# Nearest-neighbour upsampling on one core: the first load's issue moves from SyncE's DMA queue to ScalarE's

## The chip, the cores and the metric

The kernel runs on one core of one Trainium2 chip. The metric is the device time of one execution in microseconds (us). The kernel before takes 197.63 us, the median of three runs (197.22 to 197.87).

On this core SP (SyncE) and ACT (ScalarE) issue the DMAs of this kernel. The page of the profile lists two DMA queues: q1 carries ten DMAs, as many as SP issues, and q10 two, as many as ScalarE issues. Both are served by the same 16 DMA engines. VectorE (DVE) and ScalarE do the copying inside on-chip memory. TensorE (PE) has no work.

## The reference

Every pixel of a float32 image batch of shape 16 x 64 x 64 x 64 is repeated twice in both directions:

```python
for i in range(new_h):
    for j in range(new_w):
        src_i = i // scale_factor      # scale_factor is 2
        src_j = j // scale_factor
        result[:, :, i, j] = x[:, :, src_i, src_j].copy()
```

16.78 MB are read and 67.11 MB are written.

## The kernel before

The image rows of all batches and channels are one list of 16 x 64 x 64 = 65,536 rows of 64 floats. Each of the 128 partitions holds 512 of them, which follow each other in memory, so one partition's share is 128 KB of input and 512 KB of output. The whole input stays on chip in `xt`, the rear part of one large tile `mem` (lines 186 to 188).

Three loads bring the input, cut by rows (lines 192 to 195): rows 0 to 31 (the "head", 8 KB in a partition), rows 32 to 287 (64 KB) and rows 288 to 511 (56 KB).

The loop in lines 204 to 217 then goes over nine chunks of rows, of 54, 38, 54, 61, 54, 63, 63, 63 and 62 rows. For each chunk

- VectorE expands the first `kv` rows into a buffer inside `mem` (line 213) and ScalarE the others (line 214). In chunk 0 VectorE has 53 rows, so its copy reads rows 0 to 52, and ScalarE only row 53.
- one DMA stores the chunk (line 216). SP issues it, but chunks 3 and 5 are issued by ScalarE (line 215).

The buffers alternate between the front of `mem` and the region just below the rows not yet expanded, which reaches into rows of `xt` that are done with. A buffer is used again once its store has landed, and a region of `xt` once its rows have been expanded. The framework adds the waits for this from the reads and writes; a DMA announces that it has landed through a semaphore.

Every engine first runs a short opening block which ends in a barrier that all engines pass together, and then the body. Two functions edit the finished program. `begin_before_barrier` (line 13) takes SP's first `EARLY` = 3 instructions of the body, which are the three loads, and puts them ahead of SP's drain in the opening block, so that SP issues them before it arrives at the barrier. `close_early` (line 80) rearranges the block at the end, so that only SP waits for the last store. `close_on_gpsimd` is defined but not used.

Of the kernel before, what the change touches and what calls it, by code (L numbers as in the profile page):

```python
# [6 lines left out]

EARLY = 3  # L10


def begin_before_barrier(nc):

    blocks = nc.main_func.blocks
    main, body = blocks[0], blocks[1]
    sp = mybir.EngineType.SP
    loads = [i for i in body.instructions if i.engine == sp][:EARLY]  # L20
    for load in loads:
        assert isinstance(load, mybir.InstDMACopy), type(load)
        assert not (load.sync_info and load.sync_info.on_wait)
    names = [i.name for i in loads]
    body.instructions = [i for i in body.instructions if i.name not in names]
    kept = list(main.instructions)
    at = next(
        n
        for n, i in enumerate(kept)
        if i.engine == sp and isinstance(i, mybir.InstDrain)  # L30
    )
    kept[at:at] = loads
    main.instructions = kept


# [118 lines left out]
@with_exitstack  # L154
def kernel(
    ctx: ExitStack,
    tc: tile.TileContext,
    x: bass.AP,
    scale_factor: int,
    out: bass.AP,  # L160
):
    nc = tc.nc
    nc.at_finalize(begin_before_barrier)
    nc.at_finalize(close_early)
    P = nc.NUM_PARTITIONS
    s = int(scale_factor)
    B, C, H, W = x.shape
    R = B * C * H // P
    fdt = x.dtype

    xp = x.rearrange("b c h w -> (b c h) w").rearrange("(p r) w -> p r w", p=P)
    op = out.rearrange("b c (h hd) w -> (b c h) (hd w)", hd=s).rearrange(
        "(p r) w -> p r w", p=P
    )

    rows = [54, 38, 54, 61, 54, 63, 63, 63, 62]
    GROW = s * s
    FREE = 79
    WF = FREE * GROW * W
    assert sum(rows) == R
    mem_pool = ctx.enter_context(tc.tile_pool(name="mem", bufs=1))
    mem = mem_pool.tile([P, WF + R * W], fdt, name="mem")
    xt = mem[:, WF:].rearrange("p (r w) -> p r w", r=R)

    HEAD = 32
    cuts = [0, HEAD, R // 2 + HEAD, R]
    for lo, hi in zip(cuts, cuts[1:]):
        nc.sync.dma_start(out=xt[:, lo:hi], in_=xp[:, lo:hi])  # L195

    def expanded(r0, r1):
        return (
            xt[:, r0:r1].unsqueeze(2).unsqueeze(4).to_broadcast([P, r1 - r0, s, W, s])
        )  # L200

    r0 = 0
    before = (0, 0)
    for n, k in enumerate(rows):
        size = k * GROW * W
        at = 0 if n % 2 == 0 else WF + r0 * W - size
        assert at >= before[1] or at + size <= before[0]
        before = (at, at + size)
        u = mem[:, at : at + size].rearrange(
            "p (k a w b) -> p k a w b", k=k, a=s, w=W  # L210
        )
        kv = k - 1 if n == 0 else k * 5 // 8 & ~1
        nc.vector.tensor_copy(out=u[:, :kv], in_=expanded(r0, r0 + kv))  # L213
        nc.scalar.copy(out=u[:, kv:], in_=expanded(r0 + kv, r0 + k))  # L214
        issuer = nc.scalar if n in (3, 5) else nc.sync
        issuer.dma_start(out=op[:, r0 : r0 + k, :], in_=u)  # L216
        r0 += k
# [35 lines left out]
```

## Time and profile before

| what | value |
|---|---|
| median of three runs | 197.63 us |
| span of the profiled execution, first to last instruction | 195.7 us |
| VectorE busy | 52.3 us in 9 copies |
| ScalarE busy | 42.1 us in 9 copies and a table load |
| mean DMA rate over the span | 429 GB/s |
| SP's issue of one load | 0.38 to 0.43 us |
| first load, issue to landing | 4.7 us |
| second load, issue to landing | 23.6 us |
| third load, issue to landing | 40.2 us |
| ScalarE's own issues (chunks 3 and 5) | at 74.39 and 109.09 us |

Times inside the profile count from the span's start, which is the start of SP's issue of the first load. An issue is the instruction by which SP or ScalarE hands a transfer to its queue; the transfer starts later, and it has landed when its semaphore is complete. In the rows on windows, the columns are the stretch, its length, the busy time and number of instructions of VectorE, ScalarE and GpSimd, the granted TensorE clock, the DMA share and the GB/s. In the rows on DMA queues, a window counts the packets that start in it, with their MB and the time that they take as a share of 16 engines over the window; this can be over 100% for a short window, since a packet counts whole where it starts. So a short window's GB/s can be over what the engines move.

### The profile page before, as it was taken

What the parts mean: (1) busy time and instruction counts of PE and PEld (TensorE: products, weight loads), DVE (VectorE), ACT (ScalarE), POOL (GpSimd) and SP (SyncE); (2) the same over time, 40 slices, a digit from 0 to 9 for tenths busy, and PEclk for the clock granted to TensorE, in tenths of its full rate; (3) what the DMA queues carried; (4) which work ended last, traced back from release to release, by engine and by line L of the source; (5) the groups of instructions that cost most, each with busy time, mean ns of one, the idle gap of its engine ahead of it and who ended that gap; (6) DMA issues with size and microseconds to landing.
All of it is one profiled execution on the core that took longest, in us unless ns stands there. A gap on an engine that the chain in (4) does not pass through costs nothing.

```text
span 195.7 us, 102 instructions
## 1 busy us (share of the span) xinstructions
DVE 52.3 (27%) x9; ACT 42.1 (21%) x10; POOL 0.2 (0%) x4
## 2 busy tenths in 40 slices
DVE  0000099940026081000627200055540063000000
ACT  2000000150029700000694000059700073000000
POOL 0000000000000000000000000000000000000000
DMA  9999989889898989989999899999999999999994
GB/s 429 429 429 429 402 375 562 375 362 542 362 435 382 540 384 441 490 385 406 408 476 475 362 482 488 416 422 422 422 422 422 422 422 422 435 499 493 428 441 208
DMA packets 1728, 83.89 MB, mean 429 GB/s; under 512 B 192, under 2 KB 192, under 8 KB 192
## 3 DMA queue, kind: packets, MB, share of 16 engines
q1 hardware_dynamic: 1440, 67.63, 80.1%
q10 hardware_dynamic: 288, 16.25, 19.2%
HBM read 16.78 MB, written 67.11 MB: 429 GB/s over the span
## 4 chain that ended last, share of the span: by engine, by line
DMA 65%; ACT 11%; DVE 7%; SPq 0%; issue 0%; DVEq 0%; ACTq 0%
DMA out_dram<-mem 53%; DMA mem<-in_x_dram 12%; ACT mem L214 11%; DVE mem L213 7%; SPq L195 0%; DVEq L213 0%; ACTq L214 0%; SPq L216 0%
## 5 line engine op out<-in xcount | busy, mean ns | idle before, releaser
L213 DVE COPY mem<-mem 128x9728 f32<-128x9728 f32 (+3 forms) x9 | 52.3, 5818 | 111.0 <-DMA out_dram<-mem 86.9
L214 ACT COPY mem<-mem 128x6400 f32<-128x6400 f32 (+5 forms) x9 | 40.8, 4530 | 119.6 <-DMA out_dram<-mem 84.4
L214 ACT ACT_TABLE_LOAD x1 | 1.3, 1283 | 1.7 <-PEq L234 1.7
L234 POOL MEMSET const-bfloat16-1.0<- 128x1 bf16 x1 | 0.1, 101 | 0.0
L234 POOL MEMSET const-uint8-127<- 128x1 uint8 x1 | 0.1, 101 | 0.0
L234 POOL MEMSET const-float32-0.0<- 128x1 f32 x1 | 0.1, 98 | 0.2 <-issue 0.2
L234 POOL MEMSET const-float32-1.0<- 128x1 f32 x1 | 0.1, 98 | 0.0
## 6 DMA issues: line engine op xcount, KB each, us to landing
out_dram<-mem SPq DMA_DIRECT2D x3, 6912.0 KB, 30.1
out_dram<-mem SPq DMA_DIRECT2D x2, 8064.0 KB, 27.8
out_dram<-mem ACTq DMA_DIRECT2D x1, 8064.0 KB, 29.9
out_dram<-mem SPq DMA_DIRECT2D x1, 7936.0 KB, 32.3
out_dram<-mem ACTq DMA_DIRECT2D x1, 7808.0 KB, 29.3
mem<-in_x_dram SPq DMA_DIRECT2D x1, 7168.0 KB, 40.2
out_dram<-mem SPq DMA_DIRECT2D x1, 4864.0 KB, 26.8
mem<-in_x_dram SPq DMA_DIRECT2D x1, 1024.0 KB, 4.7
```

The lines of the kernel that those rows point to most:

```text
L213: nc.vector.tensor_copy(out=u[:, :kv], in_=expanded(r0, r0 + kv))
L214: nc.scalar.copy(out=u[:, kv:], in_=expanded(r0 + kv, r0 + k))
L234: nc = _bacc.Bacc("TRN2", target_bir_lowering=False, num_devices=1)
```

## The change

The first of the three loads is issued by ScalarE in place of SP. `EARLY` becomes a table with a number of loads for each of the two engines, and `begin_before_barrier` moves ScalarE's first DMA of the body ahead of ScalarE's drain in the opening block, and SP's first two ahead of SP's. The sizes of the loads, the copies and the stores stay as they are.

```diff
-EARLY = 3
+EARLY = {mybir.EngineType.Activation: 1, mybir.EngineType.SP: 2}
...
     main, body = blocks[0], blocks[1]
-    sp = mybir.EngineType.SP
-    loads = [i for i in body.instructions if i.engine == sp][:EARLY]
...
     kept = list(main.instructions)
...
+    for engine, early in EARLY.items():
+        loads = [
+            i
+            for i in body.instructions
+            if i.engine == engine and isinstance(i, mybir.InstDMACopy)
+        ][:early]
+        for load in loads:
+            assert not (load.sync_info and load.sync_info.on_wait)
+        names = [i.name for i in loads]
+        body.instructions = [i for i in body.instructions if i.name not in names]
+        at = next(
+            n
+            for n, i in enumerate(kept)
+            if i.engine == engine and isinstance(i, mybir.InstDrain)
+        )
+        kept[at:at] = loads
     main.instructions = kept
...
     for lo, hi in zip(cuts, cuts[1:]):
-        nc.sync.dma_start(out=xt[:, lo:hi], in_=xp[:, lo:hi])
+        issuer = nc.scalar if lo == 0 else nc.sync
+        issuer.dma_start(out=xt[:, lo:hi], in_=xp[:, lo:hi])
```

More of the change, by code (lines that the diff above doesn't have):

```diff
@@ L18, in begin_before_barrier @@
     main, body = blocks[0], blocks[1]
-    sp = mybir.EngineType.SP
-    loads = [i for i in body.instructions if i.engine == sp][:EARLY]
[L21 to L25, printed above, removed]
-    kept = list(main.instructions)
[L27 to L32, printed above, removed]
+    kept = list(main.instructions)
+    for engine, early in EARLY.items():
[14 more added lines that the diff above has]
+        kept[at:at] = loads
     main.instructions = kept
```

## The prediction

> **What bounds the kernel now.** I read the chain of waits first, because it says which kind of work leads from the start to the end.
>
> ```profile
> 24.11 14.30 DVE mem L213
> 38.41 0.02 issue
> 38.42 0.02 SPq L216
> 38.44 0.04 issue
> 38.48 18.96 DMA out_dram<-mem
> ```
>
> (Start in us, length in us, what.) The chain begins with SP's second load, issued at 0.43 and landed 23.58 us later, at 24.01. VectorE's first copy starts at 24.11 and ends at 38.41, SP issues the first store at 38.48, and from there to the end the chain changes between stores and short copies.
>
> Second, the page's rows on the DMA queues: is there idle DMA time that an earlier or later load could use up?
>
> ```profile
> DMA packets 1728, 83.89 MB, mean 429 GB/s; under 512 B 192, under 2 KB 192, under 8 KB 192
> ## 3 DMA queue, kind: packets, MB, share of 16 engines
> q1 hardware_dynamic: 1440, 67.63, 80.1%
> q10 hardware_dynamic: 288, 16.25, 19.2%
> ```
>
> The shares add to 99.3% of the span: the 16 engines idle 0.7% of 195.7, 1.4 us. So the kernel is bound by bytes, and a change can only cost idle time put between packets, or save what is left of the 1.4 us and of a slow ramp. The 12 DMAs have 1728/12 = 144 packets each, nine for each engine; one of the nine is tiny (192 = 12 x 16 under 512 B) and I read it as the semaphore's. q10 carries two DMAs (288/144), as many as ScalarE issues; q1 is SP's queue. A load is thus eight data packets on each engine: 8 KB for the first load (1024 KB / 128 packets), 64 KB for the second and 56 KB for the third.
>
> Third, how an engine chooses between two queues. ScalarE issues a store at 109.09, while SP's store on q1 is running. These are the packets that start in the windows 109.09 to 115.3 and 115.3 to 117.7:
>
> ```profile
> DMA packets 48, 2.80 MB, mean 451 GB/s; under 512 B 0, under 2 KB 0, under 8 KB 0
> q1 hardware_dynamic: 32, 1.77, 65.7%
> q10 hardware_dynamic: 16, 1.03, 38.3%
> ...
> q1 hardware_dynamic: 16, 0.88, 85.0%
> ```
>
> After the issue every engine still starts two packets of q1 (32/16) beside the one that it is running, then one of q10 (16/16), then one of q1 again. ScalarE's other store shows the same: from its issue at 74.39 to 80.7, 33 packets of q1 and 16 of q10 start. So an engine is committed three packets deep, the running one and two more, and then alternates packet by packet.
>
> **The change part by part.** I call the 8 KB packets of the first load B1 to B8, the 64 KB ones of the second A1 to A8, the 56 KB ones of the third C1 to C8; b and a are the semaphore's packets.
>
> Issuing. SP's three issues take 381 to 432 ns each. SP now issues two, so its barrier comes 0.4 us earlier and ScalarE's 0.4 us later than they did (ScalarE's drain stood at 0.1, SP's first issue at 0.00). The barrier released ScalarE at 1.73, and nothing behind it is needed before 24.0. If that cover were gone the sum would be 0.4 us. ScalarE's queue q10 holds nothing else before the store issued at 74.39, and GpSimd's carries none of the DMAs, so no transfer is passed there. No wait is added: VectorE's first copy already waits for two loads. Price: nothing.
>
> First packet. In the first 1.0 us no packet starts; six start in the next 0.1. This delay is now that of A1, issued at 0.00, instead of B1: nothing either way. The window rows show a slow ramp behind it:
>
> ```profile
> 1.00:1.50 0.50, 0.00 (x0) 0.00 (x0) 0.00 (x0) 1.00 1.37 328
> 1.50:2.00 0.50, 0.00 (x0) 0.27 (x1) 0.00 (x0) 1.00 0.77 229
> 2.00:3.00 1.00, 0.00 (x0) 1.00 (x1) 0.00 (x0) 1.00 0.97 410
> 78.80:91.60 12.80, 0.00 (x0) 0.00 (x0) 0.00 (x0) 1.00 1.00 435
> ```
>
> (Last column GB/s.) Against 435 the first two microseconds lose 156/435 + 25/435 = 0.42 us. If 64 KB packets ramp better, between 0 and 0.4 us is saved. The last row is also a stretch in which both queues alternate: interleaving costs no rate.
>
> The order of the first 9 MB: here is the cost. ScalarE's issue starts at 0.1 if it takes the place of its drain, behind SP's A at 0.00, and SP's C follows A at about 0.43. If an idle engine fills its three places as soon as A is there, A1, A2 and A3 are committed before B can be seen. Then it alternates:
>
> A1 A2 A3 B1 A4 B2 A5 B3 A6 B4 A7 B5 A8 B6 a B7 C1 B8 C2 b
>
> Before, b and a both stood ahead of C1. Now two packets of the third load stand ahead of b. The third load landed at 0.9 + 40.2 = 41.1, the second at 24.0, so a C packet takes 17.1/8 = 2.1 us, and the first load lands 2 x 2.1 = 4.2 us later than the second did, at 28.2. VectorE's first copy (53 rows) needs rows of both loads, so it starts at 28.3 rather than 24.11, ends 14.30 later at 42.6, and the first store is issued at 42.7 rather than 38.48. ScalarE's first copy needs row 53 alone, from the second load; its next copy waited 14.0 us for VectorE and slips with it. Nothing else is queued on VectorE.
>
> What the 4.2 us cost. Some of it is covered: the first store was issued at 38.48, but the engines only came free for it between 40.1 and 40.8 (32 packets start in that window, 16 of them tiny). On idle engines its packets would have started after 38.48 + 1.0, by the delay of the first load, which gives 0.6 us of cover on the earliest engine. If a store's first packet comes faster, the cover grows; at no delay it is 40.1 - 38.5 = 1.6. The loads themselves end as early as before, since the bytes ahead are the same. So the idle time is 4.2 - 0.6 = 3.6 at most and 4.2 - 1.6 = 2.6 at least. I take 3.2, nearer to the first, as the only idle start in the trace is the loads'. Afterwards nothing gives it back: from 41 to 195 the window row reads 430 GB/s, so every later store slides by the same amount, with the copies between them.
>
> Sum: 195.7 + 3.2 = 198.9 for the span. The profiled execution's span lies 1.9 below the median of 197.63; I add the same 1.9: **200.8 us**, with 200.2 to 201.2 as this case's own range.
>
> Against this stands the Trainium skill. The page "DMA: Bandwidth & Descriptors", section "Issuing engines are not separate DMA queues", says that issuing from several engines saves only the sequencer's time to issue, since all transfers interleave on the same 16 engines. By that alone the sum would be the 197.4 of the rival below. The trace agrees that rate is unchanged (435 GB/s with both queues), but shows that interleaving moves a transfer's landing.
>
> **The rivals.**
>
> *Order does not bite* (not slower). If B reaches an engine before A, or no more than one A packet ahead of it is taken, the order is B1 A1 B2 A2 or A1 B1 A2 B2, and a and b both still come ahead of C1. Landing stays at 24.0, and half of the 0.4 us ramp gives 197.63 - 0.2 = 197.4. It decides as soon as the three-deep commitment is not filled within the 0.1 us by which SP leads. For it: the lead is tiny; the rows show commitment only on busy engines. Also, what I read as depth might be a delay of some 4 us until a new queue is noticed. Against that: load 1 needed 1.0 us, and both stores found two packets per engine though the engines' packet starts are spread over 2 us.
>
> The same page, section "Queues, rings and completion order", has an engine drain a whole packet of about 9 to 17 descriptors from a ring before it switches. If that packet were all eight of a load's pieces, A would be finished, then B, then C, and the forecast would be this rival's. The trace does not agree: q10 and q1 take turns after 16 pieces, one on each engine.
>
> *Two packets ahead instead of three.* If A1 and A2 alone are taken, b stands behind one C packet: 2.1 us late, less 0.6 to 1.6 of cover: 0.5 to 1.5, about 1.0, so 198.6.
>
> *The load comes much later.* If the first use of ScalarE's queue costs some microseconds, or the move ahead of the barrier does not do what it says and ScalarE issues behind the release at 1.73, the three-deep commitment holds all the more: A4 is chosen when A1 ends, about 3.4. Only a load seen later than that lands another 2.1 us late per A packet: 202.9.
>
> *Ramp and finish gain.* The ramp's whole 0.42 is saved, and the engines finish together: their last tiny packets start between 194.7 and 195.4, some 0.6 us apart, so up to 0.3 more on the average. 197.63 - 0.7 = 196.9. [...] Against it: the same cold start is paid by A1, and the rows do not show that packet size causes it.
>
> **How the numbers follow.** Three ahead 0.5, two ahead 0.13, much later 0.07, order does not bite 0.2, ramp gain 0.1. A difference counts from 0.3%, 0.6 us, about what a measurement of this kernel can tell from no change (its runs lie between 197.22 and 197.87). Slower is the first three, 0.7; same 0.2; faster 0.1. The time is that of the likeliest case, 200.8. The range reaches down to the unchanged order with its whole ramp gain, 197.63 - 0.42 = 197.2, and up to the 3.6 us bound and the 0.2 by which the slowest run lies above the median, 201.4. It leaves out the last rival and the much later load, 0.17.
>
> **What would show it.** On the changed kernel's windows of the first 30 us: q10's first 8 KB packets behind 48 packets of q1 (three on each engine), its tiny packets near 28 rather than ahead of 23.7; VectorE's first copy at about 28.3, released by the load; the first store's issue at 42.7; and a hole in the DMA row between about 40.5 and 43.5. If VectorE still starts near 24.1, commitment was not deep at an idle start, and I am wrong. If it starts late but the DMA row has no hole, the cover was larger than I took. If the times after the hole do not shift by one amount, later stores gave something back.

## The result: 0.16% slower, with the order unharmed

| | before | changed |
|---|---|---|
| median of 21 runs each | 197.47 us | 197.75 us |
| ratio, 95% interval | | 1.0016 (1.0010 to 1.0022) |
| profiled execution, span | 195.7 us | 196.7 us |

The forecast was 200.8 and slower. The kernel is 0.28 us slower, less than the 0.3% that was to count. What happened is the first rival, "order does not bite", without the small gain that it included.

The chain of waits of the changed kernel (start, length, what):

```profile
0.11 24.35 DMA mem<-in_x_dram
24.47 0.02 issue
24.49 14.30 DVE mem L217
...
38.86 18.87 DMA out_dram<-mem
```

It begins with ScalarE's load, issued at 0.11, which lands at 24.46 and releases VectorE at 24.49, 0.38 later than the 24.11 of before. The forecast had 28.3 here, and 42.7 for the store that is issued at 38.86.

The rows on the queues over the whole span:

```profile
DMA packets 1728, 83.89 MB, mean 427 GB/s; under 512 B 192, under 2 KB 192, under 8 KB 192
...
q1 hardware_dynamic: 1296, 66.59, 78.8%
q10 hardware_dynamic: 432, 17.30, 20.4%
```

The 144 packets of the first load have moved from q1 (1440) to q10 (288). The change does what it says. 78.8 + 20.4 = 99.2%: no hole. The packets that start from 3.9 to 4.9 us show why:

```profile
q1 hardware_dynamic: 16, 1.05, 241.8%
q10 hardware_dynamic: 16, 0.13, 30.9%
```

Between 1.0 and 2.0 every engine has begun its first 64 KB packet A1 (the last fence of this section). From 2.0 to 4.3 nine packets of q10 start and none of q1, and from 3.9 to 4.9 there are 16 of each, one for each engine. From 4.9 to 7.1 come the next of q10:

```profile
q10 hardware_dynamic: 10, 0.08, 8.8%
q1 hardware_dynamic: 1, 0.07, 6.9%
```

I read the order as A1 B1 A2 B2, with no second A ahead of B1. The share gives the length of a packet: for the second A packets, 241.8% of 16 engines over 1.0 us, on 16 packets, is 2.42 us each. The same row for 1.0 to 2.0:

```profile
q1 hardware_dynamic: 16, 1.05, 312.9%
```

The first sixteen take 3.13 us each, 0.71 more than the ordinary 2.42. Before, with 8 KB packets first, the ramp cost 0.42 (from the GB/s of its first two microseconds). The difference of 0.29 is most of the 0.38 by which VectorE starts later. ScalarE's first copy, which needs the 64 KB load alone, starts at 24.32 rather than 24.03, also 0.29 later.

### The profile page after: what moved, and what is told of

Read it like the earlier page. It is cut to its first block, busy times and chain, and to the rows that moved or that the text cites. A ratio compares the mean times of both kernels' runs of the same rounds, so it can differ in the third digit from the quotient of the medians.

```text
span 196.7 us, 102 instructions
## 1 busy us (share of the span) xinstructions
DVE 52.3 (27%) x9; ACT 42.1 (21%) x10; POOL 0.2 (0%) x4
## 3 DMA queue, kind: packets, MB, share of 16 engines
q1 hardware_dynamic: 1296, 66.59, 78.8%
q10 hardware_dynamic: 432, 17.30, 20.4%
## 4 chain that ended last, share of the span: by engine, by line
DMA 66%; ACT 10%; DVE 7%; issue 0%; ACTq 0%; SPq 0%
DMA out_dram<-mem 53%; DMA mem<-in_x_dram 12%; ACT mem L218 10%; DVE mem L217 7%; ACTq L218 0%; SPq L220 0%
```

## The experiments

In the table, "before" is the kernel before, run on the same chip as its row. The lead is the time from SP's first issue to ScalarE's issue of its load, from the timeline. The ratio and its interval come from all executions and are not exactly the quotient of the two medians.

| run | load order and lead | median, before's | ratio (95%) | VectorE starts |
|---|---|---|---|---|
| changed | A on SP, B on ScalarE, 0.11 | 197.75, 197.47 | 1.0016 (1.0010 to 1.0022) | 24.49 |
| e12 | the same, 0.33 | 198.65, 197.06 | 1.0078 (1.0059 to 1.0098) | 26.42 |
| e5 | the same, 0.66 | 198.60, 197.12 | 1.0071 (1.0050 to 1.0093) | 26.38 |
| e3 | the same, 1.25 | 198.65, 197.16 | 1.0075 (1.0062 to 1.0089) | 26.46 |
| e6 | the same, 2.76 | 200.82, 197.12 | 1.0183 (1.0164 to 1.0202) | 28.59 |
| e2 | B and C on SP, A on ScalarE, 0.12 | 200.87, 197.16 | 1.0189 (1.0174 to 1.0205) | 28.56 |
| e1 | A, B, C on SP | 197.78, 197.16 | 1.0034 (1.0023 to 1.0045) | 21.83 (chunk 1) |
| e7 | half of B on each, then A, C on SP | 197.29, 197.12 | 1.0003 (0.9992 to 1.0014) | 24.25 |
| e8 | half of B, A, C on SP | 197.23, 197.12 | 1.0004 (0.9993 to 1.0015) | 24.22 |
| e4 | a head on each, then the rest on SP | 198.46, 197.16 | 1.0065 (1.0052 to 1.0078) | 13.50 |
| e11 | a head of 64 rows, then the rest on SP | 198.40, 197.15 | 1.0058 (1.0040 to 1.0076) | 7.16 |
| e9 | changed, again | 197.61, 197.15 | 1.0015 (1.0005 to 1.0025) | 24.62 |
| e10 | before, again | 197.02, 197.15 | 0.9989 (0.9979 to 1.0000) | 24.12 |

**Where does the commitment bite?** In e3 ScalarE's load stays where the framework puts it, behind the barrier.

```diff
-EARLY = {mybir.EngineType.Activation: 1, mybir.EngineType.SP: 2}
+EARLY = {mybir.EngineType.SP: 2}
```

> The 8 KB load stays on ScalarE's queue but is issued behind the barrier, some 1.2 us after SP's first issue. Theory, engines commit three packets once they run (the rule of the forecast, with its place wrong only at an idle start): three 64 KB packets ahead of the first 8 KB one, load lands near 28, VectorE starts near 28.3, a hole in the DMA row, about 200.8. Rival, at the first packets a newly issued load gets the next turn: VectorE at 24.5, 197.8. Between them, two packets ahead: VectorE at 26.4, 198.6.

It came out between: two packets ahead, and 198.65 where the forecast gave that case 198.6. The packets that start from 25.4 to 26.4 show what was late:

```profile
q1 hardware_dynamic: 16, 0.92, 211.6%
q10 hardware_dynamic: 16, 0.00, 0.9%
```

The 16 packets of q10 move no data that shows; they are the semaphore's, one on each engine, in the same stretch as sixteen 56 KB packets of the third load. From 3.9 to 4.9 and from 4.9 to 7.1 this run has the order of e12 below. So nothing of the 8 KB load waits behind the third load but its announcement, and that costs a whole packet, 26.46 against 24.49.

In e6 the load is later still, behind the table load, a tiny memset and a tiny copy, which write the first element of `xt` in each partition (the 8 KB load overwrites it).

```diff
-EARLY = {mybir.EngineType.Activation: 1, mybir.EngineType.SP: 2}
+EARLY = {mybir.EngineType.SP: 2}
...
+    small = xt[:, 0, 0:1]
+    nc.vector.memset(small, 0.0)
+    nc.scalar.copy(out=small, in_=small)
```

> The 8 KB load is issued by ScalarE behind its table load and one tiny copy, about 2.8 us after SP's first issue, while the first 64 KB packet is running on every engine. Theory, once packets flow the rule seen for the stores holds (the running packet and two more): three ahead, VectorE at about 28.5, first store issued at about 42.9, 200.9 as in the run with swapped loads. Rival, the depth of loads is two, whenever they come: VectorE at 26.5, 198.65.

The theory's numbers came. The chain of e6, and its window rows around the first store (stretch, length, busy time of VectorE, ScalarE and GpSimd, clock, DMA share, GB/s):

```profile
2.76 25.70 DMA mem<-in_x_dram
...
28.59 14.30 DVE mem L220
```

```profile
40.00:41.00 1.00, 1.00 (x1) 0.00 (x0) 0.00 (x0) 1.00 0.01 0
41.00:42.00 1.00, 1.00 (x1) 0.00 (x0) 0.00 (x0) 1.00 0.00 0
42.00:43.00 1.00, 1.00 (x2) 0.04 (x1) 0.00 (x0) 1.00 0.00 0
43.00:44.00 1.00, 1.00 (x1) 1.00 (x1) 0.00 (x0) 1.00 2.08 885
```

The load lands at 28.46 and VectorE starts at 28.59. No data packet starts from 40 to 43; the load packets begun before 40 run out meanwhile, the first store is issued at 42.96, and its first 16 packets, one for each engine, start from 43.8 to 44.0. This is the hole that the forecast described. Not all engines had three packets ahead: from 4.9 to 7.1, seven packets of q10 had started, so some engines had taken only two. The slowest sets the landing.

e5 and e12 put empty drains ahead of ScalarE's early load, 16 and 6 of them. They serve only to pass time, about 0.035 us each by the leads of the two runs.

```diff
-        kept[at:at] = loads
+        kept[at:at] = pause + loads     # pause: empty drains, on ScalarE alone
```

> The changed kernel with 16 empty drains on ScalarE ahead of its load, so that SP leads by some tenths of a us more than 0.1. Theory, an engine fills its places one after the other during the start (one 64 KB packet taken by a lead of 0.1, two by a lead of 1.25): either still one ahead, VectorE at 24.5 and 197.8, or already two, VectorE at 26.5 and 198.65; the lead at which it turns lies between 0.1 and 1.25. Rival, only the barrier or the body matters and not the lead: as the changed kernel whatever the lead.

> The changed kernel with 6 empty drains ahead of ScalarE's load, a lead of about 0.3 us. Sixteen gave a lead of 0.66 and two packets ahead (198.6), none gives 0.11 and one ahead (197.7). If the second place is filled soon after the first, it is taken already: VectorE at 26.4, 198.6. If it is filled later than about 0.3, VectorE at 24.5 and 197.7. If the engines differ, the slowest decides: VectorE at 26.4.

Both had two packets ahead. The rows of e12 for 3.9 to 4.9 and for 4.9 to 7.1 stand against the changed kernel's:

```profile
q1 hardware_dynamic: 16, 1.05, 241.9%
...
q1 hardware_dynamic: 10, 0.66, 68.7%
q10 hardware_dynamic: 16, 0.13, 14.0%
```

From 3.9 to 4.9 each engine starts a second 64 KB packet and no packet of q10; the 8 KB packets start behind it. So 0.2 us more of lead on one queue costs a whole packet: the second 64 KB packet goes ahead from a lead between 0.11 and 0.33, the third, on some engines, from one between 1.25 and 2.76.

The prediction had another reading of its rows, a delay of some 4 us until a new queue is noticed. A fixed delay doesn't fit these runs. In the changed kernel and in e6 the first packet of q10 starts less than 4.0 and 3.8 us after its issue (before 4.1 and 6.5). In e12 six packets of q1 and none of q10 start from 4.4 to 4.6, at least 4.0 us after the issue at 0.33. In e2 (next) all of q10's first sixteen have started by 3.1, under 3.0 us after the issue.

**The two loads swapped (e2).** SP issues the 8 KB load and the third, ScalarE the 64 KB load.

```diff
-        issuer = nc.scalar if lo == 0 else nc.sync
+        issuer = nc.scalar if lo == HEAD else nc.sync
```

> SP issues the 8 KB load and the third, ScalarE the 64 KB load 0.1 us later. Theory of the ramp of large first packets: an 8 KB packet is first on every engine, so the ramp is like before and the time 197.5, if the queues take turns from the first packet. Rival of two queues that start together: about 197.75. If the engines commit several packets of SP before they see ScalarE's, one or more of the 64 KB packets stands behind the third load's and VectorE starts 2.1 us or more later: 198.2 to 200.8.

```profile
0.12 28.41 DMA mem<-in_x_dram
28.53 0.02 issue
28.56 14.30 DVE mem L217
...
42.93 17.77 DMA out_dram<-mem
```

The chain shows the third outcome. With the same lead of 0.12 the engines took several of SP's small packets first: up to 2.15 us, 37 packets of q1 had started and none of q10. The landing is 4.1 us later than the changed kernel's, the time of two packets of the third load. The landing at 28.53, the store's issue at 42.93 and the 200.87 are close to the forecast's 28.2, 42.7 and 200.8, in a kernel for which it was not made. The first outcome, 197.5, asked for turns from the first packet on, and there were none. So the lead alone does not set how many packets go ahead: at 0.11 to 0.12 it is one of 64 KB in the changed kernel, but two or more of 8 KB on the average here and in e4 (60 of q1 before 2.6 us) and five of 4 KB in e7 (85 before 2.4). Here and in those two, q10's first packet starts 2.0 us or more after its issue. What makes an engine choose its next packet, a number of places, bytes or a time, no run here shows.

**What costs the 0.28?** e1 keeps all loads on SP and only puts A first. If the ramp theory holds, it is as slow as the changed kernel.

```diff
-    for lo, hi in zip(cuts, cuts[1:]):
-        issuer = nc.scalar if lo == 0 else nc.sync
-        issuer.dma_start(out=xt[:, lo:hi], in_=xp[:, lo:hi])
+    for lo, hi in zip((HEAD, 0, R // 2 + HEAD), (R // 2 + HEAD, HEAD, R)):
+        nc.sync.dma_start(out=xt[:, lo:hi], in_=xp[:, lo:hi])
```

> All three loads on SP's queue, the 64 KB one first, then the 8 KB one, then the third; ScalarE issues no load. Theory, the small loss of the changed kernel is the ramp of large first packets: as slow as the changed kernel, about 197.75 (0.15% over before), the semaphore packets of the first 9 MB near 23.4 to 23.9 in place of 23.1 to 23.7. Rival, the loss comes from two queues that start together: as before, 197.5, semaphore packets at 23.1 to 23.7.

From 1.0 to 2.0 us:

```profile
q1 hardware_dynamic: 15, 0.98, 300.2%
```

300.2% x 16 / 15 is 3.20 us a packet, on one queue. The time rose by 0.34%, somewhat more than expected; here the framework also let VectorE do chunk 1 first, so that the first store was issued at 39.20, and that may be part of it. e7 is the other half of the test: two queues at once, but small packets first on both.

```diff
-    cuts = [0, HEAD, R // 2 + HEAD, R]
+    cuts = [0, HEAD // 2, HEAD, R // 2 + HEAD, R]
...
-        issuer = nc.scalar if lo == 0 else nc.sync
+        issuer = nc.scalar if lo == HEAD // 2 else nc.sync
```

> The 8 KB load is halved: rows 0 to 15 lead SP's queue, rows 16 to 31 ScalarE's, the other two loads stay on SP's; VectorE's first copy still needs the 64 KB load. Theory of the ramp of large first packets: small packets first on both queues, so the ramp of before, 197.2 to 197.5, and not the 0.3 us more of the changed kernel. Rival of two queues that start together: about 197.8.

No loss that can be measured. So large first packets cost time on one queue alone, and two queues with small first packets lose 0.14% at most, just under the changed kernel's 0.15 and 0.16%. That speaks for the size of the first packets as the cost, and not the second queue. e8 halves the first load on SP's queue alone (16 rows, the second load 272).

> All three loads on SP's queue as before, but the first has 16 rows (4 KB packets) and the second 272. Theory of the ramp: what counts is how much comes in small packets while the ramp lasts, to about 2 us; with half as many bytes in them the 64 KB packets begin inside the ramp and the loss lies between before and the changed kernel, 197.5 to 197.8. Rival, only the very first packet of an engine counts, smaller is better: as before or up to 0.2 faster.

Its 1.0004 (0.9993 to 1.0015) excludes a loss over 0.3 us but does not tell the two theories apart well; that the ramp's length decides is not shown.

**Two versions that change more than the ramp.** e4 gives ScalarE rows 0 to 31 and SP rows 32 to 63 ahead of the rest; e11 gives SP a first load of 64 rows. In both, VectorE no longer needs the large load.

> Four loads: ScalarE rows 0 to 31, SP rows 32 to 63, 64 to 287, 288 to 511, all ahead of the barrier; so both queues begin with 8 KB packets. Theory of the ramp of large first packets: the ramp of before or a better one, 197.2 to 197.5. Rival of two queues that start together: about 197.75.

> All loads on SP's queue, the first with 64 rows (16 KB packets), so that it brings all that VectorE's first copy needs. Theory of the ramp by packet size: between 8 KB (0.42 us lost) and 64 KB (0.7): 197.1 to 197.5 from the ramp alone. VectorE starts near 7 us rather than 24 and the first store is issued near 22; as the DMA engines have no idle time to fill, nothing is gained by that, and stores that begin beside the loads may lose what the run with two heads lost (198.5).

e4's expectation overlooked that the first copy would no longer wait for the large load, so it does not test the ramp. VectorE started at 13.5 and 7.16, the first stores were issued at 27.87 and 21.54, and the kernels were slower by 0.6%. The load packets that start in e11 from 38.1 to 38.7, the last of the third load:

```profile
q1 hardware_dynamic: 16, 0.92, 558.3%
```

and in the kernel before from 37.9 to 38.5:

```profile
q1 hardware_dynamic: 16, 0.92, 369.3%
```

558.3% of 0.6 us is 3.35 us a packet (e4 has 3.34), against 2.22 before. Where the store already waits in the queue behind the loads, the last load packet of every engine takes 1.1 us longer, which is most of the 1.25 lost. In the changed kernel, where the store is issued after all of these packets have started (38.86), they take 2.12. That the waiting store is the cause is read from these four kernels; no run holds the store back alone.

**Again, both kernels (e9, e10).**

> The changed kernel once more, for a second profile. Theory of the ramp: its first 64 KB packets take about 3.1 us rather than 2.4 again, the times 0.1 to 0.4% over before. If the stores from 100 to 150 us lose a further few tenths of a us as in its first profile (430 GB/s against 438), that loss belongs to the kernel; if they don't, it belonged to that execution.

> The kernel before as a control, for a second profile: ratio 1.000 within 0.1%. If its stores show the loss of the changed kernel's profile this time, that loss varies from execution to execution and explains its two groups of times, near 197.0 and 197.6.

The loss came again, and again smaller than that between two single profiles (196.3 and 195.6 here). The profiles hold a second piece: the packets that start from 74 to 194 us, all of them stores, of the kernel before:

```profile
q1 hardware_dynamic: 656, 36.14, 69.5%
q10 hardware_dynamic: 288, 16.25, 31.2%
```

and of the changed kernel:

```profile
q1 hardware_dynamic: 656, 36.14, 69.8%
q10 hardware_dynamic: 288, 16.25, 31.3%
```

The same packets take 0.4% of 120 us longer, 0.5 us. The second profiles repeat it (101.0% in all for the changed kernel, 100.7% for the one before), and e1 has 101.0%, e7 100.9%. So both profiles of the changed kernel have it. Whether the kernel before has it in some executions, as the expectation allowed, was not seen: a time is 1.3 to 1.4 us over its profile's span, so the two profiles of before belong to times near 197.0, and none was taken of those near 197.6. That would also explain why two profiles differ by more than the medians.

Large first packets alone don't explain it: e2 starts with 8 KB packets, and its stores (all packets from 43 to 199.4 us) keep the 16 engines for 99.3% of 156.4 us, 155.3 us. The kernel before has 155.0 (99.6% from 40.12 to 195.7), the changed one 155.4 (99.5% from 40.37 to 196.6). Why stores are slower after some starts stays open: no run here took a cause away.

None of the versions beats the kernel before.

## Why the prediction was wrong

- *What bounds the kernel.* Right. Bytes bound it, and e4 and e11, where VectorE starts 10.6 and 17 us earlier, gained nothing.
- *Issuing and barrier.* Right. ScalarE issued at 0.11, the barrier released it at 1.25 rather than 1.73, and nothing came of it.
- *The order of the first 9 MB.* This step failed, in the clause "if an idle engine fills its three places as soon as A is there, A1, A2 and A3 are committed before B can be seen". The rows behind it were of busy engines. At an idle start the 64 KB packets are not taken three at once: one went ahead at the lead of 0.11, two from 0.33 to 1.25, three at 2.76, and then not on all engines. The small packets of e2 show that a lead is not the whole rule. The rival named the very point ("is not filled within the 0.1 us by which SP leads") and got 0.2; the lead was read rightly from ScalarE's drain and should have weighed more.
- *"The three-deep commitment holds all the more"* for an issue behind the barrier. Wrong too: e3 has two.
- *The price of a late landing.* Right in kind, where it was paid. Two C packets late: forecast VectorE 28.3, store 42.7; e6 has 28.59 and 42.96, and the hole. The cover was taken from a first packet 1.0 us after its issue; e6's store has 0.8 to 1.0. The size was too low: 3.7 against its own before rather than 3.2, above the bound of 3.6, and for one late packet (e3, e5, e12) 1.5 to 1.6 rather than 1.0. The 0.3 of the ramp and the slower stores are in that, and the forecast had neither.
- *From the span to the time.* The 1.9 was too much. e6's time is 1.3 over its span (200.78 and 199.5), e10's 1.4. The profile of before is of an execution some 0.6 under the median of 197.63 that it was held against. So that 200.82 meets the forecast's 200.8, and 198.60 to 198.65 its 198.6, is luck: two errors of about 0.6 cancel (span 199.5 against 198.9).
- *The ramp.* The sign was wrong. I bounded it between 0 and 0.4 saved and gave no bound below nothing; large first packets cost 0.71 rather than 0.42, 0.3 lost.
- *The rule against the change.* The Trainium skill ("DMA: Bandwidth & Descriptors", section "Issuing engines are not separate DMA queues") has several issuers save issue time only. For the changed kernel its outcome came: no landing moved by a packet, and 197.75 is near the 197.4. e3, e6 and e12 show that the same two queues cost 1.5 to 3.7 us when the second is issued a little later.

## What to carry to other kernels

Spreading loads over two queues adds no rate, but it decides which load lands first, in whole packets; with 64 KB packets 0.2 us of lead moved a landing by 2 us and the kernel's time by about 1.2. Keep what is needed first in one queue and in order, or see that the last piece of each needed load, its semaphore's packet, stands ahead of anything later. Begin a cold DMA stream with small packets; here that was worth 0.3 us.

## What I had not expected of the hardware

- A depth that was measured on busy engines did not hold at their start: the second 64 KB packet went ahead from between 0.11 and 0.33 us of lead, the third only from between 1.25 and 2.76, and on some engines.
- The packet of a semaphore takes its own turn: in e3 it alone stood behind a 56 KB packet of the other queue, and the load was announced 2 us later for it.
- The first 64 KB packet of an idle engine took 3.13 us, later ones 2.42; with 8 KB packets first the ramp lost 0.42 us rather than 0.71.
- Where stores were queued behind loads on one queue, the last 56 KB load packet took 3.35 us in place of 2.22 (e11, e4), the cause not tested alone.
- The same stores took 0.3 to 0.5 us more in about 155 in the changed kernel and in e2 than in the kernel before, cause open.
